# A smaller second selection, 16-bit look-ups, and 56 dense key rows for 64 in a one-core decoder layer

## The chip, the cores and the metric

The kernel runs on one core of a Trainium2 chip. Its time is the device time of one execution in microseconds (us). TensorE is the matmul engine; VectorE (DVE), ScalarE (ACT) and GpSimd (POOL) work beside it, SyncE (SP) issues plain transfers, and GpSimd issues the indirect ones (gathers by a list of row numbers).

## The reference

One post-norm decoder layer on 256 tokens of 2048 numbers: a projection, eight differential and eight stick-breaking attention heads, an output projection and a layer norm; then PEER, a retrieval of single-neuron experts; then a gated embedding. The change is in PEER:

```python
sa = jnp.einsum('thc,nc->thn', qa, sub_keys[0])        # 128 scores, first half key
sb = jnp.einsum('thc,nc->thn', qb, sub_keys[1])
va, ia = lax.top_k(sa, 16)
vb, ib = lax.top_k(sb, 16)
cand = va[..., :, None] + vb[..., None, :]             # 16 x 16 sums
top, sel = lax.top_k(cand, 16)                         # over 256 candidates
eidx = ia*128 + ib of the 16 chosen                    # expert number, 0..16383
gates = softmax(top)
act = gelu(einsum('thed,td->the', u[eidx], x))         # 8 heads x 16 experts a token
out = einsum('the,thed->td', gates * act, v[eidx])
```

`u` and `v` have 16384 rows of 2048 numbers (8 KB each), all of it in 32-bit floats.

## The kernel before, in words

**Two ways through PEER.** The first 88 tokens (64 + 16 + 8, `GROUPS`) are done "sparse": each of their experts' rows is gathered, 128 rows (1 MiB) to a gather, 88 gathers of `u` rows and 88 of `v` rows. VectorE forms the dot products (L986) and sums (L996). The other 168 tokens (`NDT`) are done with matmuls over blocks of 128 experts. An expert's number is ia*128 + ib, and the ia (key rows) are cut in two parts, `PARTS`: rows 0 to 63 are part 0, rows 64 to 127 part 1.

**The stages, in order of time.** (1) *query*: 16 products with `peer_wq`, scores, and the top 16 of the first token half (`topk_heads(0, ...)`), a head at a time. (2) *dense u*: for each of the `SEG1` = 64 key rows of part 0, `u_block` multiplies the whole 128-expert block of `peer_u` with the 168 tokens (L217) and keeps the gelu in `A0`/`A1`. Beside it the second token half's top 16 is found, the experts in use are counted (`first_flags`, `second_flags`, `count`), and lists of used experts are made (`list_work`). (3) *sparse u*: the used experts of part 1 are gathered by list, 128 to a block, transposed on TensorE (L1335) and multiplied (L1344). `CAPS` says how many blocks there are: 27 narrow ones, for experts that only the second half uses (128 columns), and 16 wide ones (168 columns). (4) *v*: the used experts of part 0 (27 + 17 blocks) and then of part 1 (27 + 16) are gathered from `v_rows` into `vf`, their weights from the table `s_w` into `wc` (L1305), and multiplied (`v_mm`, L1390). (5) *the seam and tail*: held blocks, the sparse tokens' sums brought in (`third_sums`, L1054; `v_out`, L1404; `res2`, L1462), the norm, the gate and the output.

**The gate pass.** `gate_work` builds, for three tokens at a time, one-hot matrices of ia and ib and multiplies them to a gate matrix per token (`product`, L1088 and L1089). The gates are scaled and split in two 16-bit parts: `hi` on ScalarE (L1079), `lo` on VectorE (L1080). Part 0's result multiplies `A0`/`A1` in place, which are then spilled to the table `s_w0`; the pass runs under sparse u. Part 1's result `G2` is made under part 0 of v, spilled to `s_w1`, and multiplied in `weigh` (L1413) with the gelu `WL`. A part-1 block's `wc` can be gathered only once `s_w1` is written (`done`). `G2` opens in the memory that `A0` and `A1` leave.

**What sets the order.** Side work is written as generators that yield; `run(work, n)` takes n steps between matmul blocks. `steps` is n in dense u. `gathers(n)` adds n to a sum and issues one sparse gather for each whole one, so the constants are gathers per block: `GQ` in query, `GU` in dense u until `second_flags` starts, `GUF` after it, `GUT` in its last ten blocks, `GUL` (narrow, wide) in sparse u, `GV` (narrow, wide) in v. Four buffers `gb` take the gathers. Reads of `wf`, `uf` and `vf` share five 1 MiB buffers, and row blocks are fetched up to `LEAD` = 4 blocks ahead. What a planner may not move is wrapped in `keep`; the rest it orders by its own model of durations.

**The first top 16 and the look-ups.** Per head, `top16` takes two MAX8, two FIND_INDEX8 and one MATCH_REPLACE8 over the 256 sums. The chosen position is split in i and j by shift and mask; then, per head and side, VectorE compares the positions with 0..15 (L731), GpSimd multiplies with the index list (L734), and VectorE adds up (L742, L744).

## Time and profile before

| | us |
|---|---|
| median of 3 runs | 1714.49 (1713.68 to 1715.63) |
| the profiled execution | 1712.57 |
| its span, first to last instruction | 1710.8 |
| TensorE busy / VectorE busy | 1612.1 / 1094.6 |
| query / dense u / sparse u | 414 to 534 / 534 to 853 / 853 to 1112 |
| v / seam and tail | 1112 to 1555 / 1555 to the end |

Durations are of the one profiled execution. A row of a group shows the count, the union of busy time and the mean of one in ns, then the engine's idle time just before these instructions and what ended it. Matmuls overlap, so the mean of one is longer than its step from start to start. A 32-bit matmul is two instructions.

### The profile page before, as it was taken

The page shows a single profiled execution, that of the slowest core. Times are in us where ns is not written, and L with a number is a line of the kernel's source. Part 1 is how long each engine was busy: PE and PEld are TensorE (multiplying, and loading weights), DVE is VectorE, ACT ScalarE, POOL GpSimd, SP SyncE. Part 2 cuts the span into 40 slices and gives each one's busy share as a digit, 9 for nine tenths or more (in the row PEclk, how much of TensorE's full clock was granted, in tenths as well). Part 3 has the DMA queues.
Part 4 walks back from the last instruction along what each step waited for, and adds up shares of the span by engine and source line. Part 5 has one row for each costly group of instructions (what it writes and reads, how often), then busy time and mean ns, then how long its engine had stood idle before and what let it go on. Part 6 is the DMA issues. An engine that isn't in the chain of part 4 may idle for free.

```text
span 1710.8 us, 29575 instructions
## 1 busy us (share of the span) xinstructions
PE 1612.1 (94%) x11176; PEld 1489.4 (87%) x11176; DVE 1094.6 (64%) x2430; ACT 717.9 (42%) x1666; POOL 718.1 (42%) x612
## 2 busy tenths in 40 slices
PE   9999999999999999999999999988897698984998
PEld 7888888877889999999999999978897688984786
DVE  5565488763599996656666867358672344544676
ACT  5677468753112654866366665313220000000552
POOL 0143023103266235111544655478886668871000
PEclk9999999999999999999999999989999899996999
DMA  7645644484998998988999999989999899996561
GB/s 294 197 151 166 234 154 160 159 315 156 379 361 319 379 364 344 408 334 310 364 421 391 350 344 345 412 348 373 398 409 413 319 419 414 387 413 230 175 262 50
DMA packets 94089, 531.26 MB, mean 311 GB/s; under 512 B 13257, under 2 KB 16649, under 8 KB 41465
## 3 DMA queue, kind: packets, MB, share of 16 engines
q0 software_dynamic: 49600, 329.36, 49.0%
q1 hardware_dynamic: 42612, 196.79, 31.3%
q10 hardware_dynamic: 1728, 3.15, 0.5%
q8 instruction: 90, 1.47, 0.3%
q14 instruction: 59, 0.48, 0.1%
HBM read 515.75 MB, written 16.08 MB: 311 GB/s over the span
## 4 chain that ended last, share of the span: by engine, by line
PE 71%; DMA 16%; issue 6%; POOL 3%; DVE 2%; ACT 1%; POOLq 0%; ACTq 0%; DVEq 0%; SPq 0%
PE ps_u L217 18%; PE ps_u L1344 8%; PE ps_qk L205 7%; DMA gb<-v_rows,eig 7%; PE ps_q L217 6%; PE ps_v L1390 5%; DMA vf<-v_rows,idxV 5%; PE ps_T L1335 4%; PE ps_qk L207 4%; DMA s_w<-A 2%; PE ps_v L224 2%; PE ps_v L226 2%; PE ps_v L225 2%; POOL wc L1305 2%; PE ps_gate L224 1%
## 5 line engine op out<-in xcount | busy, mean ns | idle before, releaser
L1390 PE MATMUL ps_v<-wc,vf 128*128 128x128 f32 (+1 forms) x2784 | 374.0, 295 | 57.6 <-DMA vf<-v_rows,idxV 26.0
L1390 PEld LDWEIGHTS ps_v<-wc,vf 128*128 128x128 f32 x2784 | 360.9, 197 | 64.4 <-DVE wc L1413 23.0
L217 PE MATMUL ps_u<-XF,wf 128*128 128x168 f32 x1888 | 291.4, 311 | 0.0
L996 DVE SCALAR_TENSOR_TENSOR y<-gb,ew,y 128x2048 f32<-128x2048 f32 x78 | 183.1, 2347 | 158.4 <-DMA gb<-v_rows,eig 158.3
L127 DVE TENSOR_TENSOR wl<-wf,wh 128x1024 fp32r<-128x1024 f32 (+1 forms) x199 | 212.7, 1091 | 104.3 <-ACT wh L126 103.1
L217 PEld LDWEIGHTS ps_u<-XF,wf 128*128 128x128 f32 x1888 | 271.4, 190 | 3.6
L126 ACT CAST wh<-wf 128x1024 fp32r<-128x1024 f32 (+1 forms) x199 | 172.1, 892 | 231.6 <-DMA wf<-ple_gate 117.6
L986 DVE SCALAR_TENSOR_TENSOR gb<-gb,xq 128x2048 f32<-128x2048 f32 x88 | 202.1, 2301 | 25.4 <-DMA gb<-u_rows,eig 22.7
L1344 PE MATMUL ps_u<-XF,uT 128*128 128x128 f32 (+1 forms) x1376 | 199.7, 289 | 0.0
L1020 POOL DMA_INDIRECT gb<-u_rows,eig x88 | 108.8, 1237 | 197.8 <-DVE eqb L857 69.7
L205 PE MATMUL ps_qk<-X,wh 128*128 128x512 f32 x512 | 185.2, 401 | 0.0
L1344 PEld LDWEIGHTS ps_u<-XF,uT 128*128 128x128 f32 x1376 | 178.9, 191 | 0.2
L1020 POOL DMA_INDIRECT gb<-v_rows,eig x88 | 134.9, 1533 | 58.7 <-issue 18.1
L207 PE MATMUL ps_qk<-X,wl 128*128 128x256 f32 x512 | 145.7, 285 | 0.0
L1079 ACT ACTIVATE hi<-eq,ghf 128x64 f16<-128x64 f16 x336 | 92.3, 339 | 121.5 <-DVE eq L857 111.1
L1338 ACT COPY uT<-ps_T 128x512 f32<-128x512 f32 x172 | 100.5, 586 | 97.9 <-PE ps_T L1335 95.1
L1305 POOL DMA_INDIRECT vf<-v_rows,idxV x87 | 118.6, 1363 | 48.6 <-issue 19.3
L1305 POOL DMA_INDIRECT wc<-s_w,idxW x87 | 117.6, 1351 | 40.7 <-issue 24.3
L205 PEld LDWEIGHTS ps_qk<-X,wh 128*128 128x128 f32 x512 | 96.4, 188 | 22.0 <-issue 1.0
L217 PE MATMUL ps_q<-XF,wf 128*128 128x256 f32 x512 | 113.8, 379 | 0.6 <-ACT eb L586 0.6
L217 PEld LDWEIGHTS ps_q<-XF,wf 128*128 128x128 f32 x512 | 95.8, 190 | 13.3 <-ACT eb L586 1.0
L1335 PE MATMUL ps_T<-ident,uf 128*128 128x128 f32 x688 | 103.8, 275 | 0.0
(342 smaller groups left out, 2550.9 us busy)
## 6 DMA issues: line engine op xcount, KB each, us to landing
wf<-peer_u SPq DMA_DIRECT2D x59, 1024.0 KB
wf<-w_qk SPq DMA_DIRECT2D x64, 512.0 KB
wf<-w_out SPq DMA_DIRECT2D x32, 512.0 KB
wf<-peer_wq SPq DMA_DIRECT2D x16, 1024.0 KB
wf<-ple_gate SPq DMA_DIRECT2D x16, 1024.0 KB
wf<-w_v SPq DMA_DIRECT2D x16, 512.0 KB
wf<-w_sv SPq DMA_DIRECT2D x15, 512.0 KB
s_w<-G SPq DMA_DIRECT2D x8, 672.0 KB
```

The source lines that it names most:

```text
L126: self.order(nc.scalar.copy(wh, src))
L127: self.order(nc.vector.tensor_tensor(wl, src, wh.bitcast(F32), op=ALU.subtract))
L205: nc.tensor.matmul(ps, wh[:, j * P:(j + 1) * P], xt[:, dt, :], start=dt == 0, stop=False)
L207: nc.tensor.matmul(ps[:, :T], wl[:, j * P:(j + 1) * P], xt[:, dt, :T], start=False, stop=dt == ND - 1)
L217: nc.tensor.matmul(ps[:, :T - t0], wf[:, dt * P:(dt + 1) * P], xt[:, dt, t0:], start=dt == 0, stop=dt == ND - 1)
L986: keep(nc.vector.scalar_tensor_tensor(g, g, 1.0, xq[i], op0=ALU.mult, op1=ALU.mult, accum_out=eact[i][:, j:j + 1]))
L996: keep(nc.vector.scalar_tensor_tensor(ys[i], g, ew[i][:, j:j + 1], ys[i], op0=ALU.mult, op1=ALU.add))
L1020: keep(nc.gpsimd.indirect_dma_start(out=g, out_offset=None, in_=a[kind], in_offset=bass.IndirectOffsetOnAxis(ap=eig[i][:, 0, j:j + 1], axi ...
L1305: keep(nc.gpsimd.indirect_dma_start(out=dst, out_offset=None, in_=src, in_offset=bass.IndirectOffsetOnAxis(ap=idx[:, b:b + 1], axis=0), bo ...
L1335: nc.tensor.transpose(ps[:, j * P:(j + 1) * P], uf[:, (4 * c + j) * P:(4 * c + j + 1) * P], ident)
L1344: nc.tensor.matmul(ps[:, :n], uT[:, j * P:(j + 1) * P], XF[:, d, NSP + c0:NSP + c0 + n], start=d == 0, stop=d == ND - 1)
L1390: return nc.tensor.matmul(o, vf[:, d * P:(d + 1) * P], wc[:, c0:c0 + n], start=False, stop=last and (d % 3 == 2 or d == ND - 1))
```

## The change

It has five parts.

1. Second selection: `a[i] + b[j]` of two sorted lists of 16. If (i+1)*(j+1) > 16, sixteen or more sums are at least as large, so only i < 3 with any j, and the other i with j < 4, are kept: 3 x 16 + 13 x 4 = 100 sums for 256. The position is decoded with shifts and a maximum.
2. Look-ups: for several heads in one go, in 16-bit floats, on VectorE alone: compare, multiply, and four adds that halve the list. The first token half is done in `BATCH`es of 1, 2, 2, 2, 1 heads for 8 single ones, the second all at once (29 yields for 34).
3. Counts: the count's bank is zeroed by a matmul first, so the first half's counts may be added at any time and run on beside the second half's. `steps` is 4 for 5, then 3.
4. The `lo` products of three tokens become one 16-bit operation.
5. Sizes and schedule: 56 dense key rows for 64; the part sizes and block counts that follow; part 1's gate pass is made ready at block 43 of sparse u's 48 and steps on there; in v the pass always takes 2 steps per half block; gather rates are changed; `wc` has 5 slots for 8 in part 0.

```diff
-SEG1 = 64
+SEG1 = 56
...
-CAPS = ((27, 17), (27, 16))
+CAPS = ((24, 15), (30, 18))
...
+CAND = ((0, 3, 16), (3, 16, 4))
+NCAND = sum((i1 - i0) * w for i0, i1, w in CAND)
+BATCH = ((0, 1), (1, 2), (3, 2), (5, 2), (7, 1))
...
-GQ = 1.6
-GU, GUF, GUT = 0.60, 0.85, 0.50
-GUL, GV = (0.95, 1.30), (0.62, 0.92)
+GQ = 1.7
+GU, GUF, GUT = 0.80, 0.92, 0.50
+GUL, GV = (1.00, 1.40), (0.66, 0.95)
...
+    def equal(dst, keys, vals, order=keep):
+        n, m = dst.shape[1], dst.shape[2]
+        shape = [P, n, m // 2, 2]
+        order(nc.vector.tensor_tensor(
+            dst.rearrange("p n (k two) -> p n k two", two=2),
+            pairs(keys)[:, None].to_broadcast(shape), vals[:, :, None, :].to_broadcast(shape),
+            op=ALU.is_equal))
...
+        for i0, i1, w in CAND:
+            shape = [P, n, i1 - i0, w]
+            c1 = c0 + (i1 - i0) * w
+            first(nc.vector.tensor_tensor(
+                cand[:, :n, c0:c1].rearrange("p h (i j) -> p h i j", j=w),
+                a[:, :, i0:i1, None].to_broadcast(shape), b[:, :, None, :w].to_broadcast(shape),
+                op=ALU.add))
+            c0 = c1
         for h in range(h0, h0 + n):
...
+            top16(tkl, CV[:, t, h, :], CI[:, t, h, :], cand[:, h - h0, :], first)
+            yield
...
+        for which, dst in ((0, iaN), (1, ibN)):
+            eq = tkl.tile([P, PH * TOPK, TOPK], F16, name="eqsel", tag="eqsel", bufs=1)[:, :nk]
+            equal(eq, io128[:, :TOPK], at[which], first)
+            e4 = eq.rearrange("p (h k) i -> p h k i", k=TOPK)
             first(nc.vector.tensor_tensor(
+                e4, e4, TIh[:, t, 2 * h0 + which:2 * h0 + 2 * n:2, None, :].to_broadcast(
+                    [P, n, TOPK, TOPK]), op=ALU.mult))
+            if n > 2:
+                yield
+            for w in (8, 4, 2):
+                first(nc.vector.tensor_tensor(eq[:, :, :w], eq[:, :, :w], eq[:, :, w:2 * w],
+                                              op=ALU.add))
+            first(nc.vector.tensor_tensor(dst[:, t, h0 * TOPK:(h0 + n) * TOPK], eq[:, :, 0],
+                                          eq[:, :, 1], op=ALU.add))
             yield
...
-        keep(nc.tensor.matmul(cnt[0][:, h * P:(h + 1) * P], ohb, eq, start=t in (NSP, P),
-                              stop=t in (P - 1, T - 1)))
+        keep(nc.tensor.matmul(cnt[0][:, h * P:(h + 1) * P], ohb, eq, start=False,
+                              stop=t == T - 1))
...
+        keep(nc.tensor.matmul(cnt[0], ident, zero.to_broadcast([P, 2 * P]), start=True,
+                              stop=False))
...
             next(gating, None)
+            next(flags, None)
             yield
...
-                keep(nc.vector.tensor_scalar(lo[:, j, :], eq[:, j, :], glf[:, t], None,
-                                             op0=ALU.mult))
+            shape = [P, n, ns // 2, 2]
+            keep(nc.vector.tensor_tensor(
+                lo[:, :n].rearrange("p n (k two) -> p n k two", two=2),
+                eq[:, :n].rearrange("p n (k two) -> p n k two", two=2),
+                gl2[:, t0:t0 + n, None, :].to_broadcast(shape), op=ALU.mult))
...
-        gathers(1 if ia < EARLY else GU if steps == 1 else GUF if ia < SEG1 - 10 else GUT)
+        gathers(0.9 if ia < EARLY else GU if steps == 1 else GUF if ia < SEG1 - 10 else GUT)
...
-        wc = wpool.tile([P, NDT], F32, name="wc", tag="wc", bufs=NWC)
+        wc = wpool.tile([P, NDT], F32, name="wc", tag="wc", bufs=LEAD + 1 if wpool is wcp else NWC)
...
             wcp = pools.open("wcp", "right", bufs=1)
+            work = gate_work(ohp, (G2,), *PARTS[1], 1, True)
...
-            if 2 <= b < NBLK[1] - 5 and (c or n > P):
+            if b >= 2 and (c or n > P):
                 run(work, 1)
...
-    work = gate_work(ohp, (G2,), *PARTS[1], 1, True)
...
-            done = run(work, 2 if n > P or d > 8 else 1)
+            done = run(work, 2)
```

More of the change, by code (lines that the diff above doesn't have):

```diff
@@ L722, in topk_heads @@
-        nc.vector.tensor_single_scalar(CJ[:, t, hs], CI[:, t, hs], 15, op=ALU.bitwise_and)
-        nc.vector.tensor_single_scalar(CI[:, t, hs], CI[:, t, hs], 4, op=ALU.logical_shift_right)
-        nc.vector.tensor_copy(CIf[:, t, hs], CI[:, t, hs])
-        nc.vector.tensor_copy(CJf[:, t, hs], CJ[:, t, hs])
-        yield
-        late = []
-        for which, pos, dst in ((0, CIf, iaN), (1, CJf, ibN)):
-            for h in range(h0, h0 + n):
-                eq = tkl.tile([P, TOPK, TOPK], F32, name="eq", tag="eqsel", bufs=4)
-                first(nc.vector.tensor_tensor(
-                    eq, pos[:, t, h, :, None].to_broadcast([P, TOPK, TOPK]),
-                    io128f[:, None, :TOPK].to_broadcast([P, TOPK, TOPK]), op=ALU.is_equal))
-                nc.gpsimd.tensor_tensor(
-                    eq, eq, TIf[:, t, 2 * h + which, None, :].to_broadcast([P, TOPK, TOPK]),
-                    op=ALU.mult)
-                late.append((dst[:, t, h * TOPK:(h + 1) * TOPK], eq))
-                if h % 2:
-                    yield
-                if len(late) > 2:
-                    o, e = late.pop(0)
-                    nc.vector.tensor_reduce(o, e, axis=AX.X, op=ALU.add)
@@ L743, in topk_heads @@
-        for o, e in late:
-            nc.vector.tensor_reduce(o, e, axis=AX.X, op=ALU.add)
-        yield
+        a, b = (TV[:, t, 2 * h0 + which:2 * h0 + 2 * n:2] for which in range(2))
+        cand = tkl.tile([P, PH, NCAND], F32, name="cand", tag="cand", bufs=1)
+        c0 = 0
+        for i0, i1, w in CAND:
[6 more added lines that the diff above has]
+            c0 = c1
@@ new lines, in topk_heads @@
+        for h in range(h0, h0 + n):
+            top16(tkl, CV[:, t, h, :], CI[:, t, h, :], cand[:, h - h0, :], first)
+            yield
+        ci = CI[:, t, hs].rearrange("p h k -> p (h k)")
+        s4, s2 = (tkl.tile([P, PH * TOPK], U32, name=nm)[:, :nk] for nm in ("by16", "by4"))
+        pF, u1 = (tkl.tile([P, PH * TOPK], F32, name=nm)[:, :nk] for nm in ("pF", "u1"))
+        at = [tkl.tile([P, PH * TOPK, 2], F16, name=f"at{which}")[:, :nk] for which in range(2)]
+        two = [P, nk, 2]
@@ new lines, in topk_heads @@
+        first(nc.vector.tensor_copy(TIh[:, t, 2 * h0:2 * h0 + 2 * n],
+                                    TI[:, t, 2 * h0:2 * h0 + 2 * n]))
+        first(nc.vector.tensor_single_scalar(s4, ci, 4, op=ALU.logical_shift_right))
+        first(nc.vector.tensor_single_scalar(s2, ci, 2, op=ALU.logical_shift_right))
+        first(nc.vector.tensor_copy(pF, ci))
+        first(nc.vector.scalar_tensor_tensor(
+            at[0], s2[:, :, None].to_broadcast(two), -9.0, s4[:, :, None].to_broadcast(two),
+            op0=ALU.add, op1=ALU.max))
@@ L798, in topk_work @@
         nc.vector.tensor_copy(io128, io128f)
-        for h in range(PH):
-            for _ in topk_heads(0, h, 1):
-                pass
-            head_slots(h)
+        for h0, n in BATCH:
+            for _ in topk_heads(0, h0, n):
+                pass
+            for h in range(h0, h0 + n):
+                head_slots(h)
             yield
@@ L807, in topk_work @@
         second, first, flags = topk_heads(1, 0, PH), gates(0), first_flags()
-        for step in range(24):
-            next(second)
+        for step, _ in enumerate(second):
             if step > 2:
@@ L813, in topk_work @@
             yield
-        for _ in second:
-            next(flags, None)
-            yield
-        for _ in range(9):
-            next(flags, None)
-            yield
-        for _ in flags:
-            yield
+        for _ in first:
+            pass
         yield from index_T(1)
-        yield from second_flags(gates(1))
+        yield from second_flags(gates(1), flags)
     def index_T(t):
@@ L922, in second_flags @@
                 counts()
+        for _ in flags:
+            yield
         while made:
@@ L1189, in list_work @@
         if part:
-            steps = 5
+            steps = 3
         yield
@@ L1268, in build @@
             iaT, ibT = (lsp.tile([P, T, 2], F16, name=nm) for nm in ("iaT", "ibT"))
[L1269 removed]
+            ghf = lsp.tile([P, T], F32, name="ghf")
+            gl2 = lsp.tile([P, T, 2], F16, name="gl2")
             a0p = pools.open("a0p", "right", bufs=1)
@@ L1276, in build @@
         query(hh)
-        if hh % 2 == 0 and hh:
+        if hh in [2 * (h0 + n) for h0, n in BATCH]:
             run(work, 1)
```

40 lines of the change are left out of this document (17 added, 23 removed).

## The prediction

> **What bounds the kernel now.** I read the page first: the busy shares and the slices.
>
> ```profile
> span 1710.8 us, 29575 instructions
> ...
> PE 1612.1 (94%) x11176; PEld 1489.4 (87%) x11176; DVE 1094.6 (64%) x2430; ACT 717.9 (42%) x1666; POOL 718.1 (42%) x612
> ...
> PE   9999999999999999999999999988897698984998
> ...
> PEclk9999999999999999999999999989999899996999
> DMA  7645644484998998988999999989999899996561
> ```
>
> TensorE is full up to slice 26; nearly all of its idle time lies in slices 26 to 37. The DMA engines are nearly full from slice 10 on. So the list of what TensorE waited for says which of the two is short there:
>
> ```profile
> PE ps_v L1390 <- DMA vf<-v_rows,idxV: 26.0, 15, 5.1
> PE ps_v L1390 <- DVE wc L1413: 18.6, 5, 12.9
> PE ps_y L1462 <- DVE XF L1404: 17.2, 2, 16.1
> PE ps_G L1088 <- DVE lo L1080: 6.4, 1, 6.4
> PE ps_v L1390 <- issue: 5.5, 5, 1.5
> PE ps_v L1390 <- PEq L1521: 4.5, 1, 4.5
> ```
>
> All six belong to the second half of the retrieval: v blocks (L1390), the gate pass under them (L1088) and their end (L1462). By stage (columns: stretch, length, busy time of PE, weight load, DVE, ACT, POOL, then granted clock, DMA share, GB/s; query, dense u, sparse u, v in two pieces, the seam to the tail):
>
> ```profile
> 414.00:534.00 120.00, 119.39 (x591) 105.62 (x590) 84.36 (x270) 17.25 (x42) 58.48 (x62) 1.00 0.89 344
> 534.00:853.00 319.00, 319.00 (x2378) 311.62 (x2377) 236.18 (x628) 179.09 (x540) 105.44 (x133) 1.00 0.90 352
> 853.00:1112.00 259.00, 259.00 (x2397) 256.85 (x2396) 171.36 (x468) 149.98 (x388) 131.48 (x88) 1.00 0.97 378
> 1112.00:1303.00 191.00, 170.45 (x1569) 165.37 (x1568) 129.44 (x365) 46.17 (x168) 153.53 (x109) 0.97 0.97 384
> 1303.00:1555.00 252.00, 205.05 (x1526) 199.48 (x1525) 102.81 (x97) 6.72 (x12) 174.01 (x129) 0.94 0.97 393
> 1555.00:1606.00 51.00, 33.26 (x173) 30.23 (x174) 27.53 (x46) 9.02 (x20) 5.74 (x6) 0.70 0.43 134
> ...
> 1376.00:1480.00 104.00, 92.69 (x783) 90.22 (x784) 46.19 (x53) 4.54 (x8) 80.10 (x59) 1.00 1.01 415
> ```
>
> Both u stages run TensorE without a gap and have DMA share left (0.10 and 0.03). The v stage is short of DMA: share 0.97, TensorE idle 67 us of 443. So a byte moved out of v into u is worth time while u can carry it, and PE work saved in u is worth time directly.
>
> **The change, part by part.** *Blocks.* A dense block is 32 matmul instructions of 168 columns. A sparse block is 16 transposes and 32 instructions, in 128 (narrow) or 168 (wide) columns. From the chain of waits:
>
> ```profile
> 684.55 4.62 PE ps_u L217 x32
> 1253.44 4.64 PE ps_v L1390 x32
> 1444.85 3.81 PE ps_v L1390 x32
> ```
>
> Eight dense blocks fewer: -8 x 4.62 = -37 us. Sparse u goes from 27+16 to 30+18 blocks. The sparse stage took 259 us for 43 blocks, 6.0 each with a gate pass in it; matmuls alone bound a block below by 3.8 or 4.6. With the transposes I take 5.3 (narrow) and 6.3 (wide), as the pass must fit into the 6.0 too: 3 x 5.3 + 2 x 6.3 = +28.5. The v stage has 39+48 = 87 blocks as before, 54 narrow and 33 wide both times. Net in u: **-8 us**, 5 less MB-sized reads being 3 (8 dense, 5 row blocks).
>
> *Gathers.* Each moves 1 MiB (128 rows of 8 KB), 176 in all, and the loops hand them out at GQ, GU, GUF, GUT, GUL and GV per block. I counted the generators' yields: the step where GU ends moves from block 30 to 21. Before, issued by the end of query, dense u, sparse u: 20.8, 66.2, 112.7. After: 22.1, 67.4, 122.6. So v gets 53.4 instead of 63.4. At GV 0.66/0.95 its 39 part-0 blocks take 30.1 and 30 narrow part-1 blocks 19.8, and the rest is gone four wide blocks later: at block 73 of the 84 before the held ones. Before, 2.3 were left after block 84 and were run off in a row, which is the 16.1 us wait for XF.
>
> *Can u carry it?* Dense u moved 352 x 319 = 112 MB; eight blocks less is 104 MB in 319 - 37 = 282 us: 369 GB/s. Sparse u moved 98 MB; five more blocks and 8.7 more gathers make 112 MB in 290 us: 385 GB/s. Rows above show 378 without a gap in TensorE and 415 at share 1.01, so it fits barely. I put **+4 us** for stalls (between 0 and the 21 us of the second rival).
>
> The Trainium skill speaks against this part: its page "DMA: Bandwidth & Descriptors" (Specifications) gives about 358 GB/s as the HBM limit of one core, below the 435 of the fabric. By that, u's 216 MB would take 603 us and not 572, an estimate of 31 us lost. The 415 GB/s of the row above disagrees, so I don't use it.
>
> *v stage.* Before: 384 x 191 + 393 x 252 = 172 MB. After: 10 gathers less (10.5 MB) and 0.7 MB more table (72 rows for 64): 162 MB. From block 73 on v is bound by TensorE: 11 wide blocks x 4.64 = 51 us. By then the reads are five blocks ahead, so all but some 13 MB (9 blocks of 1.14 MB, and weights of the next stage) came before it, at 405 GB/s, between the 393 and 415 of the rows: 149 / 405 = 368 us. Sum 419, against 443 now: -24. The same sum gives 426 for before, where 443 was measured, so 17 us there were not bandwidth. They are the late second pass: its 64 x 168 table is spilled only when v block 38 or so ends, and part 1's wc gathers can't start before. The pass needs 125 yields; 20 now run in u, and at 4 a block the rest ends near v block 26, eight blocks ahead of its first reader. I leave 6 of the 17: v **-18 us**.
>
> *Seam.* The rest of the XF wait goes too, less 2 us for the first result: **-14**. Behind it TensorE ran at 0.70 of its clock for 51 us:
>
> ```profile
> 1571.00 0.69 PE L1462 MATMUL ps_y<-ident,XF 128*128 128x128 f32 x2 [16.10 <-DVE XF L1404]
> ...
> 1571.69 13.49 PE ps_y L1054 x64
> ```
>
> 64 small matmuls took 13.5 us there. With the array kept busy the seam's 33 us of PE work at 0.70 would be about 25: **-8**. If the branch check (PEq, 4.5 us, stays) already lowers the clock, 0.
>
> *VectorE.* Its rows for what goes, and for what is like the new forms:
>
> ```profile
> L680 DVE MAX8 CV<-cand 128x8 f32<-128x256 f32 x16 | 6.8, 428 | 0.3
> ...
> L680 DVE MAX8 TV<-S 128x8 f32<-128x128 f32 x32 | 9.1, 284 | 24.8 <-ACT S L701 24.8
> ...
> L731 DVE TENSOR_TENSOR eq<-CJf,io128f 128x256 f32<-128x256 f32 x16 | 10.1, 637 | 0.0
> ...
> L742 DVE TENSOR_REDUCE iaN<-eq 128x16 f32<-128x256 f32 x8 | 3.2, 406 | 0.0
> ...
> L857 DVE TENSOR_TENSOR ohb<-io,ibT 128x384 f16<-128x384 f16 x108 | 37.7, 349 | 0.0
> ...
> L857 DVE TENSOR_TENSOR eq<-io,iaT 128x192 f16<-128x192 f16 x108 | 26.7, 247 | 0.0
> ...
> L1080 DVE TENSOR_SCALAR lo<-eq,glf 128x64 f16<-128x64 f16 x326 | 57.3, 255 | 0.0
> ```
>
> MAX8 costs 1.1 ns an element (428 and 284), so 253 ns at 100: five such operations a head save 0.9 us, 7 us per token half. Compare-and-reduce cost 16 x (0.6 + 0.4) = 16 us per half; a 16-bit operation costs 0.53 ns an element (349 and 247), so 2048 elements 1.2 us, and two rounds of compare, multiply and four adds 8 us. That is about 15 us of VectorE and 16 of POOL per half. If the multiply by a broadcast list ran at twice that, 2.4 us less. The lo products become one operation of 216 elements, 0.26 us for 3 x 0.255: 0.5 us x 112 groups = 57 us, over both passes. None of this is on the path: no TensorE wait in u names VectorE. I count it as **0**. What uses it up: the same 45 gathers, of 2.3 us each, in a dense stage 37 us shorter, and 4 pass steps per narrow v block for 3. Without that cover VectorE would be at 236 of 282 us in dense u, still under.
>
> *The rest, 0.* The bank zeroed for any-order counts is two matmul instructions (below 1 us). The first half's flags (ACT) now run partly beside the second's; see the third rival. The wc pool of part 0 has 5 slots for 8: vf has 5 too, so a pair still waits for the same block; three early wc issues of 1.35 us go, 4 us either way. Behind a waiting wc stand vf and the gathers on POOL. Part 1's first G writes, new in u, must wait for the part-0 spill reading that memory, and VectorE's gather sums stand behind them:
>
> ```profile
> 1077.26 31.47 DMA s_w<-A
> ```
>
> The spill now starts near block 39 or 40 and G2 is first written about block 44, 25 us later; the wait is 0 to some 10 us, under five blocks of prefetch, so 0.
>
> **Sum.** -8 + 4 - 18 - 14 - 8 = -44. The profiled execution took 1712.6 (span 1710.8 and 1.8 around it): 1668.6. The median of the runs is 1.9 above it, so **1670**.
>
> **Rivals.** *DMA full in u (20%).* u is bound at 365 GB/s, between its 352 and 378: 216 / 365 = 593 us, +21 for +4; v goes on at the 393 of its own row, 149 / 393 + 51 = 430, so -13 less the same 6 left over: about -7. Sum -8 + 21 - 7 - 14 - 8 = -16: 1698. For it: demand of 385 where 378 stood at 0.97. Against: 415 in the last row.
>
> *Everything fits (10%).* No stall in u, all 17 us of v's delay gone, reads at 415: -8 - 33 - 14 - 8: 1651.
>
> *The lists come late (10%, slower).* ACT's first flags take 57 us:
>
> ```profile
> L865 ACT ACTIVATE dist<-io,nibT 128x128 f16<-128x128 f16 x40 | 16.0, 401 | 1.2
> ...
> L866 ACT ACTIVATE oa<-dist 128x128 f16<-128x128 f16 x40 | 12.4, 310 | 11.2 <-PE ps_cnt L870 10.4
> ...
> L866 ACT ACTIVATE ob<-dist 128x128 f16<-128x128 f16 x40 | 12.3, 308 | 1.1
> ```
>
> (two dist each, 40 tokens: 32 + 12.4 + 12.3.) Interleaved with the second half's, they hold back the counts; the lists are in the program by block 50 of 56, a margin of 6 x 4.6 = 28 us. If the chain of counts and lists slips by the whole 57 and by the 37 of cover taken away, TensorE stands 94 - 28 = 66 us at the first row block. Against the 44 won that is +22: 1736 on the runs' scale. It decides from a slip above 72 us. Against: VectorE and ACT have 83 and 140 us idle in that stage, the second half's selection is shorter, and matmuls of u may go ahead of counts.
>
> *No change (5%).* The u stalls and the late pass eat all: within 0.2%, which is about what a measurement of this kernel can tell from no change: 1714.
>
> **How the numbers follow.** Forecast 55%, the rivals 20, 10, 10, 5. Faster 0.85, same 0.05, slower 0.10. The range takes in the second and the best case and the ends of the unknown costs (clock 0 or -8, prefetch, wc): 1647 to 1706; slower and same are mostly left out.
>
> **What would show it.** Sparse u starting near 816 us instead of 853, 290 us long, with no wait for DMA above 1 us: right in u; waits for wf or uf there: the second rival. No wait above 3 us for wc L1413 or for XF L1404, the last gather of v_rows some 50 us before the last v block, and a clock near 1 in the seam show the v and seam terms. A long wait at the first row transposes (L1335's successor) or at counts shows the lists late. I am wrong if v is not shorter although its gathers end early.

## The result, and the profile after

The changed kernel takes 1698.66 us (1696.82 to 1699.17, 4 runs) where the kernel before takes 1714.09 (1711.54 to 1715.63): a ratio of 0.991, 95% interval 0.9892 to 0.9927. It is faster, by 15.4 us; 44 had been forecast. The profiled execution took 1699.17, its span 1697.4.

The page of the changed kernel: the span, the busy shares, and three of the 40-slice rows.

```profile
span 1697.4 us, 29309 instructions
...
PE 1608.6 (95%) x11162; PEld 1485.0 (87%) x11162; DVE 1041.8 (61%) x2216; ACT 723.3 (43%) x1684; POOL 697.4 (41%) x586
...
PE   9999999999999899999999999899977988889998
...
PEclk9999999999999999999999999899998999999999
DMA  8544644484997799999899999999998999986561
```

TensorE now has short slices (14 and 26) in the two u stages, where it had none. What it waited for, from the list of waits of TensorE (us in total, times, longest):

```profile
PE ps_v L1411 <- DMA vf<-v_rows,idxV: 29.3, 15, 8.6
PE ps_v L1411 <- DVE wc L1434: 13.2, 7, 7.1
PE ps_G L1111 <- ACT hi L1099: 9.6, 2, 5.9
...
PE ps_gT L855 <- DVE iaN L774: 2.8, 1, 2.8
...
PE ps_gT L855 <- DVE ibN L774: 1.6, 1, 1.6
...
PE ps_y L1483 <- DVE XF L1425: 1.1, 1, 1.1
```

The long wait for `XF`, 16.1 us, is gone; the short one of 1.1 us behind it was there before too. New are the waits for `hi` and for the index lists `iaN` and `ibN`; the v blocks still wait for `vf` and `wc`. By stage (query, dense u, sparse u, v in two pieces, seam; columns as in the prediction's table):

```profile
414.00:537.00 123.00, 121.83 (x588) 107.52 (x589) 70.59 (x256) 17.18 (x42) 42.07 (x49) 0.97 0.85 328
537.00:829.00 292.00, 284.01 (x2123) 276.65 (x2122) 228.32 (x650) 173.49 (x533) 89.82 (x116) 0.99 0.93 365
829.00:1133.00 304.00, 293.98 (x2687) 291.25 (x2686) 186.83 (x404) 169.05 (x445) 172.20 (x111) 0.97 0.97 382
1133.00:1330.00 197.00, 170.85 (x1474) 165.15 (x1473) 106.91 (x211) 38.33 (x136) 143.79 (x104) 0.95 0.95 370
1330.00:1556.00 226.00, 197.90 (x1542) 193.01 (x1541) 87.94 (x95) 4.43 (x8) 157.65 (x119) 0.98 0.95 381
1556.00:1592.00 36.00, 34.23 (x206) 31.22 (x207) 18.08 (x42) 11.21 (x24) 2.15 (x4) 0.86 0.52 157
```

To compare kernels I cut every trace at the first matmul of each stage (first `ps_q` product, first dense `ps_u`, first `ps_T` transpose of a row block, first `ps_v` of the retrieval, first `ps_gate`), and counted the gathers that POOL had issued by the first `ps_v`. All lengths below are made in this way.

| us | query | dense u | sparse u | v and seam | rest | gathers before v |
|---|---|---|---|---|---|---|
| before | 119.4 | 318.6 | 264.1 | 489.7 | 104.9 | 108 |
| after | 122.6 | 291.3 | 307.4 | 456.3 | 105.2 | 123 |
| difference | +3.2 | -27.3 | +43.3 | -33.3 | +0.3 | +15 |
| forecast | 0 | -37 (+ part of 4) | +28.5 (+ part of 4) | -40 | 0 | +10 |

The differences sum to -13.8 (another 0.4 lies ahead of query). So the v half did most of what was forecast, and u gave 20 us of it back: it became 16 us longer and not 4.5 shorter.

### The profile page after: what moved, and what is told of

Same layout as the page of the kernel before. It is cut to its first block, busy times and chain, and to the rows that moved or that the text cites. A ratio compares the mean times of both kernels' runs of the same rounds, so it can differ in the third digit from the quotient of the medians.

```text
span 1697.4 us, 29309 instructions
## 1 busy us (share of the span) xinstructions
PE 1608.6 (95%) x11162; PEld 1485.0 (87%) x11162; DVE 1041.8 (61%) x2216; ACT 723.3 (43%) x1684; POOL 697.4 (41%) x586
## 5 line engine op out<-in xcount | busy, mean ns | idle before, releaser
L220 PE MATMUL ps_u<-XF,wf 128*128 128x168 f32 x1632 | 250.7, 310 | 0.0
L220 PEld LDWEIGHTS ps_u<-XF,wf 128*128 128x128 f32 x1632 | 235.2, 191 | 3.1 <-issue 0.2
L1368 PE MATMUL ps_u<-XF,uT 128*128 128x128 f32 (+1 forms) x1536 | 226.1, 292 | 0.4 <-ACT uT L1362 0.4
L1368 PEld LDWEIGHTS ps_u<-XF,uT 128*128 128x128 f32 x1536 | 203.2, 194 | 1.0 <-ACT uT L1362 0.7
L1040 POOL DMA_INDIRECT gb<-v_rows,eig x88 | 148.1, 1683 | 44.0 <-issue 17.9
L1362 ACT COPY uT<-ps_T 128x512 f32<-128x512 f32 x192 | 111.6, 586 | 98.8 <-PE ps_T L1359 95.7
L1099 ACT ACTIVATE hi<-eq,ghf 128x56 f16<-128x56 f16 (+1 forms) x336 | 92.3, 339 | 81.8 <-DVE eq L714 79.9
L1329 POOL DMA_INDIRECT vf<-v_rows,idxV x87 | 103.9, 1194 | 53.9 <-PE ps_v L1411 23.7
L1359 PE MATMUL ps_T<-ident,uf 128*128 128x128 f32 x768 | 115.5, 276 | 0.0
L1329 POOL DMA_INDIRECT uf<-u_rows,idxV x48 | 68.4, 1426 | 100.4 <-PE ps_T L1359 92.6
```

The source lines that it names most:

```text
L220: nc.tensor.matmul(ps[:, :T - t0], wf[:, dt * P:(dt + 1) * P], xt[:, dt, t0:], start=dt == 0, stop=dt == ND - 1)
L1040: keep(nc.gpsimd.indirect_dma_start(out=g, out_offset=None, in_=a[kind], in_offset=bass.IndirectOffsetOnAxis(ap=eig[i][:, 0, j:j + 1], axi ...
L1329: keep(nc.gpsimd.indirect_dma_start(out=dst, out_offset=None, in_=src, in_offset=bass.IndirectOffsetOnAxis(ap=idx[:, b:b + 1], axis=0), bo ...
L1359: nc.tensor.transpose(ps[:, j * P:(j + 1) * P], uf[:, (4 * c + j) * P:(4 * c + j + 1) * P], ident)
L1368: nc.tensor.matmul(ps[:, :n], uT[:, j * P:(j + 1) * P], XF[:, d, NSP + c0:NSP + c0 + n], start=d == 0, stop=d == ND - 1)
```

## The experiments

The theory after the first look: u is not short of bytes; it loses its time where VectorE, which takes its instructions in order, stands at a gather's sum with short instructions behind it that TensorE needs at once. The rivals: DMA is full in u (the second rival of the prediction), or the lists come late (the third).

**Where the gate pass starts.** The pass of part 1 put back to the start of v; and, in a second kernel, the pass left where the change has it, but no gathers handed out around its start (blocks 39 to 45 of 48).

```diff
# e1_pass_at_v
-            work = gate_work(ohp, (G2,), *PARTS[1], 1, True)
...
-            if b >= 2 and (c or n > P):
+            if 2 <= b < NBLK[1] - 5 and (c or n > P):
...
+    work = gate_work(ohp, (G2,), *PARTS[1], 1, True)
# e8_no_gather_at_seam
-        gathers(GUL[n > P])
+        if not NBLK[1] - 9 <= b < NBLK[1] - 2:
+            gathers(GUL[n > P])
```

> The changed kernel with one edit undone: part 1's gate pass is made ready when v begins, as before the change, and takes no step in sparse u. Theory A (order of queues): the two waits of TensorE for hi in sparse u (5.9 and 3.8 us) and the slow clock behind them (0.76 from 1084 to 1120) come from these steps, because VectorE stands at a gather sum when the one-hot of the pass is due. Then sparse u falls from 304 to about 290 us, and v gets a wait of some 6 us at its beginning, as the kernel before had (6.4 for lo): in all 1690 to 1699. Theory B (the DMA engines are full in sparse u): sparse u stays near 304, v gets longer by the 20 steps of the pass and the wait: 1702 to 1710.

> The changed kernel without sparse gathers beside blocks 39 to 45 of sparse u (some 10 gathers move to v). In the late-fetch run GpSimd's order did not change: five wc gathers still stood ahead of the sparse ones and waited 6.7 us for the spill, so it could not tell. Here no sparse gather is under way when the one-hots of the second pass are due. Theory A (VectorE stands at the sum of a sparse gather, and the pass behind it): the two waits of TensorE for the pass in sparse u go and sparse u falls from 306 to 293 to 297 us; v and the seam get longer by the moved gathers, as with the old rates: 1700 to 1712 in all. If the one-hots are late for another cause (ScalarE, or the spill itself before G2 is written), the waits stay and sparse u stays above 302.

Sparse u took 294.0 us in the first and 290.4 in the second (307.4 in the changed kernel; 290 was forecast). Ratios to before: 0.9856 (0.9823 to 0.989) and 0.9883 (0.9858 to 0.9908): v and the seam gave back 6.7 and 17.4 us, with 5 and 11 gathers more left for them. The timeline of VectorE in the changed kernel shows the place (start, duration, instruction, idle time before it and what ended it):

```profile
1083.97 2.35 DVE L1016 SCALAR_TENSOR_TENSOR y<-gb,ew,y 128x2048 f32<-128x2048 f32 x1 [5.79 <-DMA gb<-v_rows,eig]
...
1091.79 2.35 DVE L1016 SCALAR_TENSOR_TENSOR y<-gb,ew,y 128x2048 f32<-128x2048 f32 x1 [2.58 <-DMA gb<-v_rows,eig]
...
1094.14 0.27 DVE L714 TENSOR_TENSOR eq<-io,iaT 128x216 f16<-128x216 f16 x1
```

and of TensorE:

```profile
1085.79 2.30 PE L1368 MATMUL ps_u<-XF,uT 128*128 128x168 f32 x15
...
1094.84 0.22 PE L1111 MATMUL ps_G<-hi,ohb 128*128 128x72 f16 x1 [5.88 <-ACT hi L1099]
...
1095.80 2.61 PE L1368 MATMUL ps_u<-XF,uT 128*128 128x168 f32 x8 [0.19 <-ACT uT L1362]
```

VectorE waited for gathered rows, summed them, and only then made the one-hot `eq` (0.27 us of work) from which ScalarE makes `hi`. TensorE had the pass's product next, so u's own matmuls came behind it, and ran at half speed (8 in 2.61 us, where 15 took 2.30). The Trainium skill, "PSUM — Partial Sum Buffer" (Engine vs sequencer instructions), states that VectorE's queue is strictly first in, first out and that matmuls start in program order; the rows agree, as `eq` and u's matmuls each come right behind what was late. The window from 1084 to 1120 had a granted clock of 0.76:

```profile
1084.00:1120.00 36.00, 25.98 (x172) 24.90 (x172) 22.58 (x37) 12.87 (x37) 20.92 (x15) 0.76 0.88 350
```

These 36 us hold 10.0 us without a matmul and 36 x 0.24 = 8.6 us of clock not granted. Together that is 18.6, and sparse u is 18.3 us above the 289.1 of a kernel without the wait (f2, below). Nearly half of the price is the clock.

Without those gathers (e8) the wait is gone and the pass costs u nothing that shows. The first product of the pass in e8, on TensorE:

```profile
1087.56 0.20 PE L1111 MATMUL ps_G<-hi,ohb 128*128 128x72 f16 x1
```

That leaves POOL: five `wc` gathers stood ahead of the row gathers on its queue, the first of them waiting for the spill of `s_w0` (POOL, changed kernel).

```profile
1070.00 0.94 POOL L1040 DMA_INDIRECT gb<-v_rows,eig  x1 [0.30 <-issue]
...
1087.81 2.29 POOL L1329 DMA_INDIRECT wc<-s_w,idxW  x1 [7.16 <-DMA s_w<-A]
```

The next row gather was issued at 1098.58. By count, the sum that VectorE began at 1091.79 is of the gather issued at 1070.00, before POOL stood at the spill. So this stop can't have made the first wait; it can have had a part in the second, 3.76 us at 1109.35.

**POOL's share in it.** The `wc` gathers handed out two blocks later.

```diff
# e7_late_fetch
-        if b >= NBLK[1] - 4:
+        if b >= NBLK[1] - 2:
```

> The changed kernel with the first v block fetched two blocks later in sparse u (from block 46 of 48 for 44). In the changed kernel the first wc waits 7.2 us on GpSimd for the spill of part 0, and the sparse gathers behind it land late; VectorE stands at their sums, with the one-hot of the pass behind. Theory A: the spill has landed when wc is issued, the two waits for hi (5.9 and 3.8 us) shrink and sparse u falls by 6 to 13 us; v may begin with a wait of up to 5 us for vf: 3 to 12 us less than the changed kernel. Theory B (DMA full in sparse u): no change in sparse u, and 0 to 5 us more at the start of v.

Inconclusive: the planner still put five `wc` gathers ahead of the row gathers, POOL waited 6.65 us for the spill, TensorE 4.0 and 3.6 us; ratio 0.989 (0.9867 to 0.9912). A later run, f1_gq_160 (below), answered it: there `wc` did not wait on POOL at all, and TensorE stood as long, 9.33 us in one wait for 9.6 in two (POOL, then TensorE, of f1_gq_160).

```profile
1072.16 1.00 POOL L1329 DMA_INDIRECT wc<-s_w,idxW  x1 [0.30 <-issue]
```

```profile
1089.53 0.22 PE L1111 MATMUL ps_G<-hi,ohb 128*128 128x72 f16 x1 [9.33 <-ACT hi L1099]
```

So the spill's wait is not what makes it; VectorE's order is.

**The rates.** All five rates as before; then GU alone; then GQ alone.

```diff
# e3_old_rates
-GQ = 1.7
-GU, GUF, GUT = 0.80, 0.92, 0.50
-GUL, GV = (1.00, 1.40), (0.66, 0.95)
+GQ = 1.6
+GU, GUF, GUT = 0.60, 0.85, 0.50
+GUL, GV = (0.95, 1.30), (0.62, 0.92)
...
-        gathers(0.9 if ia < EARLY else GU if steps == 1 else GUF if ia < SEG1 - 10 else GUT)
+        gathers(1 if ia < EARLY else GU if steps == 1 else GUF if ia < SEG1 - 10 else GUT)
# e9_gu_060
-GU, GUF, GUT = 0.80, 0.92, 0.50
+GU, GUF, GUT = 0.60, 0.92, 0.50
# f1_gq_160
-GQ = 1.7
+GQ = 1.6
```

> The changed kernel with the gather rates of the kernel before (1.6; 1 for the first blocks; 0.60, 0.85, 0.50; 0.95 and 1.30; 0.62 and 0.92), everything else as changed. By the sum of the prediction some 10 gathers go back from u to v and gathers are left over at the end, so v and the seam are 18 to 30 us longer and u is at most 4 us shorter: 1712 to 1725. If DMA in u is what made u longer than forecast (theory B), u is 15 to 25 us shorter and the whole within 5 us of the changed kernel: 1694 to 1704.

> The changed kernel with 0.60 gathers per block in the first dense blocks for 0.80, every other rate as changed. With all old rates dense u had no wait and took 282 us, as forecast, and with the new ones 291 with waits for the index lists; flags started later only moved the wait (6.9 us at 647). If VectorE is full there (77 of 80 us from 575 to 655) because of the gathers brought forward, dense u falls to 282 to 284 with this one rate, and three gathers move on to later stages: 1686 to 1694 against 1695 of the changed kernel beside it. If the later rate (0.92) or the look-ups themselves are the cause, dense u stays at 289 to 292.

> The changed kernel with GQ 1.6 (rate of row gathers under the query) as before and nothing else: 22.1 - 20.8 = 1.3 gathers fewer by the end of the query stage. Theory A (the gather sums that queue on VectorE at the start of dense u stand in front of the look-ups of the last heads of the first token half, so the index lists come late): no waits for iaN or ibN above 0.5 us near 560 to 570 us, dense u 282 to 284 us for 291, ratio to the kernel before 7 to 9 us better than the changed kernel's 0.989 to 0.991, so about 0.984 to 0.986. Theory B (the dense stage is late from the rates GU and GUF of u itself): dense u stays 290 to 292 with both waits, ratio 0.988 to 0.991.

Dense u: 281.9, 290.7 and 282.9 us (291.3 in the changed kernel; 282 was forecast). Ratios 0.9929 (0.991 to 0.9948), 0.9875 (0.9848 to 0.9902) and 0.983 (0.9788 to 0.9871). One tenth of a gather per step of query, 1.3 gathers in all, costs dense u 8.4 us: TensorE's idle time in it is 8.0 us in the changed kernel and 2.7 in f1 (0.7 and 1.3 us of them waits for the second half's lists). It holds in every trace with 56 rows: 281.9 to 283.0 us in the five kernels with GQ 1.6, 288.6 to 292.0 in the eleven with 1.7. The end of the first half's look-ups in the changed kernel, on VectorE:

```profile
552.60 2.28 DVE L1006 SCALAR_TENSOR_TENSOR gb<-gb,xq 128x2048 f32<-128x2048 f32 x1
...
555.11 2.28 DVE L1006 SCALAR_TENSOR_TENSOR gb<-gb,xq 128x2048 f32<-128x2048 f32 x1
...
557.56 2.27 DVE L1006 SCALAR_TENSOR_TENSOR gb<-gb,xq 128x2048 f32<-128x2048 f32 x1
...
560.47 0.19 DVE L774 TENSOR_TENSOR iaN<-eqsel 128x16 f32<-128x16 f16 x1
...
565.34 2.29 DVE L1006 SCALAR_TENSOR_TENSOR gb<-gb,xq 128x2048 f32<-128x2048 f32 x1 [3.55 <-DMA gb<-u_rows,eig]
...
567.78 0.19 DVE L774 TENSOR_TENSOR ibN<-eqsel 128x16 f32<-128x16 f16 x1
```

and in f1_gq_160:

```profile
554.11 0.19 DVE L774 TENSOR_TENSOR iaN<-eqsel 128x16 f32<-128x16 f16 x1
...
555.69 0.18 DVE L774 TENSOR_TENSOR ibN<-eqsel 128x16 f32<-128x16 f16 x1
```

Four dot products of gathered rows, one of them late by DMA, stand inside the last batch's look-ups; `ibN` is done 12 us later than with GQ 1.6, and TensorE waits for both lists (2.76 and 1.62 us). It is the same mechanism as in sparse u. All old rates win 9 us in dense u and leave sparse u at 304.9 with 10 gathers fewer, so bytes are not what makes that stage long; in v and seam they lose 20 us (476.6).

**What v loses by.** Two kernels: part 1's `wc` pool with 5 slots for 8, as part 0 has; and a lower GV, which spreads the remaining gathers over all of v.

```diff
# e5_wc5
-        wc = wpool.tile([P, NDT], F32, name="wc", tag="wc", bufs=LEAD + 1 if wpool is wcp else NWC)
+        wc = wpool.tile([P, NDT], F32, name="wc", tag="wc", bufs=LEAD + 1)
# e6_level_v
-GUL, GV = (1.00, 1.40), (0.66, 0.95)
+GUL, GV = (1.00, 1.40), (0.55, 0.85)
```

> The changed kernel with 5 slots for wc in part 1 too, for 8. In the changed kernel eight wc gathers stand in a row on GpSimd from 1286 to 1300 when part 1's pool opens, ahead of the vf that TensorE waits 8.6 us for. Theory A (order on GpSimd's queue): with 5 slots at most five stand in a row, the 8.6 us wait and the slow clock behind it shrink: 5 to 9 us less than the changed kernel. Theory B (the DMA engines are full in v, and the order doesn't matter): within 2 us of the changed kernel.

> The changed kernel with 0.55 and 0.85 gathers per v block for 0.66 and 0.95, so that the gathers last until the end of v. In the changed kernel the DMA share is 1.01 from 1330 to 1516 and 0.66 from 1516 to 1556. If DMA bounds the middle of v, some 7 gathers moved out of it save 7 x 1.05 MB / 0.41 = 18 us there, and the later end costs part of it: 5 to 14 us less than the changed kernel. If waits for order bound v, as its length of 414 to 427 us in all kernels so far suggests, within 3 us of it. If the last gathers come too late, the seam's wait for XF returns (16 us in the kernel before).

> The changed kernel itself once more, as the measure for the runs beside it: 0.991 of the kernel before, with the same waits (5.9 and 3.8 us for hi in sparse u, 8.6 us for vf near 1310, 7.1 us for wc near 1517).

The three ran on one chip: 1687.1, 1690.24 and, for the changed kernel, 1695.22 us; ratios to before 0.985 (0.9828 to 0.9873), 0.9859 (0.9838 to 0.9879) and 0.9889 (0.9869 to 0.991). With 8 slots POOL issues eight `wc` gathers in a row when the fetches of part 1 begin, ahead of the `vf` gather that TensorE needs (POOL, first and last of the eight; then TensorE), in the changed kernel:

```profile
1286.14 1.01 POOL L1329 DMA_INDIRECT wc<-s_w,idxW  x1 [0.31 <-issue]
...
1298.43 2.44 POOL L1329 DMA_INDIRECT wc<-s_w,idxW  x1 [0.31 <-issue]
```

```profile
1310.41 3.98 PE L1411 MATMUL ps_v<-wc,vf 128*128 128x168 f32 x13 [8.60 <-DMA vf<-v_rows,idxV]
```

The changed kernel, traced again, has the same two stops of the pass in sparse u, once put down to `lo` (5.0 us) and once to `hi` (4.5). With 5 slots the wait of 8.60 is gone (the longest for `vf` is 4.0) and v and seam are 449.1 us. Levelling moves the gathers: v is 19 us shorter, the seam 13 us longer, since the last gather goes out at 1525.6 (1504.4 in the changed kernel) and a long wait for `wc`, whose multiplication stands behind the gather sums on VectorE, opens there; 450.6 together. From the waits of TensorE in e6_level_v:

```profile
PE ps_v L1411 <- DVE wc L1434: 14.8, 2, 11.7
```

How full v is, in the changed kernel, from 1330 us in three windows:

```profile
1330.00:1472.00 142.00, 121.31 (x1024) 117.75 (x1023) 59.70 (x57) 4.43 (x8) 113.39 (x82) 1.00 1.01 413
1472.00:1516.00 44.00, 37.64 (x264) 36.55 (x263) 24.57 (x28) 0.00 (x0) 34.63 (x27) 0.98 1.02 415
1516.00:1556.00 40.00, 38.95 (x256) 38.70 (x257) 3.67 (x12) 0.00 (x0) 9.63 (x11) 0.93 0.66 234
```

The DMA engines are full until the last gathers are in, and stand a third idle in the 40 us behind. Over all 18 traced kernels v and seam together fall on one line: 489.7 us with 108 gathers issued before v, 463.3 with 117, 456.3 with 123, a least-squares slope of 2.0 us per gather, with each kernel within some 7 us of the line. The kernels differ in more than the gathers, so the slope is a fit and no price measured alone: e3, e8 and e9 against the changed kernel give 2.0, 1.6 and 0.7 us per gather, f3 and f4 against f2 (below) 2.8 and 2.5. By bytes, 1.05 MB at 413 GB/s would be 2.5 us.

**The other parts.** 64 dense rows for 56, all else as changed; the first half's flags begun later; `lo` by one product a token; the old selection and look-ups.

```diff
# e4_64_rows
-SEG1 = 56
+SEG1 = 64
...
-CAPS = ((24, 15), (30, 18))
+CAPS = ((27, 17), (27, 16))
# e2_flags_later
-            next(flags, None)
+            if step > 7:
+                next(flags, None)
# e10_lo_by_one
...
-            shape = [P, n, ns // 2, 2]
-            keep(nc.vector.tensor_tensor(
...
+            for j in range(n):
+                keep(nc.vector.tensor_scalar(lo[:, j, :], eq[:, j, :], glf[:, t0 + j:t0 + j + 1], None,
+                                             op0=ALU.mult))
# e11_old_selection
-BATCH = ((0, 1), (1, 2), (3, 2), (5, 2), (7, 1))
+BATCH = tuple((h, 1) for h in range(8))
...
+                nc.gpsimd.tensor_tensor(
+                    eq, eq, TIf[:, t, 2 * h + which, None, :].to_broadcast([P, TOPK, TOPK]),
+                    op=ALU.mult)
```

> The changed kernel with 64 dense key rows and the old block counts (27+17 and 27+16), everything else as changed. By the block sum dense u is 37 us longer and sparse u 28.5 us shorter: u 8 us longer, and v starts 8 us later with as many gathers left as the rates then leave (some 4 less done in sparse u, 7 more in dense u): 1700 to 1709. Theory A adds that the part-0 pass has as little room as before (it is flushed at block 38 of 43), so TensorE's wait at the beginning of part 1's pass may be longer. If the block trade costs time, this kernel is faster than the changed one: below 1696.

> The changed kernel with the first half's flags started eight steps of the second selection later, everything else the same. Theory A: the waits of TensorE for the transposes of the index lists (2.8 and 1.6 us at 558 and 567) and the slow blocks behind them (9 and 7 us for 4.6) go, because the look-ups of the last batch are done by then: dense u 291 to about 283, 1690 to 1693 in all. Theory B (dense u is long because its transfers fill the DMA engines, share 1.01 from 575 to 655): the waits go but the time is given back at later loads: 1697 to 1701.

> The changed kernel with the old lo products (three operations of one token each, 32-bit scalars, for one operation of three tokens). The prediction counted this part at nothing: 57 us more of VectorE over both passes, under cover. If so, within 3 us of the changed kernel. If VectorE's order at the waits is what counts, the second pass starts later by some 0.5 us a group and the waits for hi and lo get longer: 3 to 10 us more.

> The changed kernel with the old second selection and look-ups (256 sums, one head at a time, 32-bit, multiplied on GpSimd), everything else as changed. The prediction counted the new ones at nothing on the path, 15 us of VectorE per token half. If VectorE is full in the first dense blocks (theory A), the 15 us come back there: the waits for the index lists and the counts grow by 10 to 25 us and the whole is 1705 to 1720. If it has room, within 4 us of the changed kernel.

With 64 rows: ratio 0.9976 (0.9956 to 0.9996); dense u 329.0, so 37.7 more than the changed kernel for 8 blocks, and sparse u 281.4 for 307.4. The trade of blocks is worth what was forecast for dense u; sparse u's share can't be read off, as that kernel has a single wait of 18.2 us for `lo` in it. Later flags: 0.9868 (0.9838 to 0.9898), dense u 290.4: the waits near 560 us are gone, but one of 6.9 us for `iaN` stands at 647, where the second half's lists are due, so the loss was only moved. `lo` one by one: 0.9907 (0.9877 to 0.9938), against 0.9889 and 0.991 for the changed kernel. Old selection: 0.9888 (0.9854 to 0.9923). Neither of the VectorE savings can be told from nothing in time. The one trace of the old selection has a sparse u of 314.2 us, with short stops for the lists at its start and one of 10.0 us for `lo`, and a dense u of 288.6.

**All causes taken out.** If these causes are separate, removing them should bring the forecast back. GQ is 1.6 and part 1's `wc` has 5 slots in all three kernels; f2 and f4 have the pass at v as e1 has, f3 has the pass in u with the gap in the gathers as e8 has.

```diff
# f2_all_causes, beside the edits of e1, e5 and f1
-GUL, GV = (1.00, 1.40), (0.66, 0.95)
+GUL, GV = (1.00, 1.40), (0.60, 0.88)
# f3_gather_gap, beside the edits of e8, e5 and f1
-GUL, GV = (1.00, 1.40), (0.66, 0.95)
+GUL, GV = (1.00, 1.40), (0.68, 0.98)
# f4_old_u_rates, beside the edits of e1, e5 and f1
-GU, GUF, GUT = 0.80, 0.92, 0.50
-GUL, GV = (1.00, 1.40), (0.66, 0.95)
+GU, GUF, GUT = 0.60, 0.85, 0.50
+GUL, GV = (1.00, 1.40), (0.64, 0.93)
...
-        gathers(0.9 if ia < EARLY else GU if steps == 1 else GUF if ia < SEG1 - 10 else GUT)
+        gathers(1 if ia < EARLY else GU if steps == 1 else GUF if ia < SEG1 - 10 else GUT)
```

> The changed kernel with every cause found so far taken out: GQ 1.6, part 1's gate pass begun at the start of v (with yields 5 and 4 to a block as in the earlier run of that kind), 5 wc slots for part 1, GV 0.60 and 0.88 between the changed kernel's 0.66 and 0.95 and the levelled 0.55 and 0.85. If the causes are separate their sizes add: dense u -8, sparse u -13, v and seam -7 (wc slots) and -3 to -5 (level), +5 for the pass put back into v: 26 to 28 us under the changed kernel, ratio 0.973 to 0.975, near the forecast's 0.974. If they share one cause (bytes: what one stage no longer waits for is waited for in the next), v grows by what u gains and the ratio stays 0.982 to 0.985.

> As the last, but with the pass left in sparse u and no gathers handed out in the seven blocks where it starts (so that no gather sum stands in front of its one-hots), GV 0.68 and 0.98 for the 7 to 8 gathers that this pushes into v. Separate causes: sparse u 290, dense u 282 to 284, v 413 to 420, seam 37 to 45: ratio 0.970 to 0.974. One shared cause (bytes): the gathers pushed out come back as v and seam longer by 12 to 17 us as in the earlier run without these gathers, ratio 0.980 to 0.985.

> As the second, but also with u's dense rates as before (0.60, 0.85, 1 in the first blocks), so 6 to 7 gathers fewer in dense u, and GV 0.64 and 0.93 for them. If GQ is what held the dense stage up: dense u 282 as in the second, v and seam 5 to 9 us longer, ratio 0.976 to 0.980. If GU or the first blocks' rate is: dense u 282 here and 290 in the second, and this one the faster of the two.

| | ratio to before | dense u | sparse u | v and seam | gathers before v |
|---|---|---|---|---|---|
| f2 | 0.9752 (0.971 to 0.9795) | 282.9 | 289.1 | 463.3 | 117 |
| f3 | 0.9838 (0.9795 to 0.988) | 283.0 | 289.3 | 480.3 | 111 |
| f4 | 0.982 (0.9778 to 0.9862) | 282.2 | 289.5 | 473.4 | 113 |

f2 is the fastest kernel of this study: 1678.62 us where before took 1720.85 in the same comparison, 42 us less (f4, the next beside it, 1689.02; the two intervals overlap a little). Its two u stages and the two pieces of v, by window:

```profile
536.00:819.00 283.00, 280.26 (x2120) 274.24 (x2118) 220.62 (x634) 172.80 (x532) 86.21 (x112) 1.00 0.93 369
819.00:1108.00 289.00, 288.87 (x2647) 285.65 (x2646) 170.68 (x363) 161.42 (x414) 159.29 (x109) 1.00 0.97 384
1108.00:1330.00 222.00, 194.14 (x1658) 187.19 (x1657) 127.77 (x259) 46.95 (x168) 166.67 (x115) 0.94 0.95 376
1330.00:1536.00 206.00, 180.83 (x1397) 176.61 (x1396) 89.49 (x95) 6.61 (x12) 150.61 (x114) 0.96 0.98 398
```

Both u stages stand at the forecast's 282 and 290, sparse u at 384 GB/s without a gap: the u causes are separate and bytes are not among them. f3 and f4 are as good in u and lose 17 and 10 us in v and seam, with 6 and 4 gathers more left for it; the line's 2.0 us each would be 12 and 8. So bytes are the one cause that is shared, as f3's expectation had it for the second case, and it acts in v. Old GU on top of GQ 1.6 (f4) wins under 1 us in dense u: GQ was what held that stage up.

That f2's 42 us are so near the forecast's 44 is in part luck. Between the traces it is 34.7 us, since the before of the same comparison ran slower than the profiled one. The split is another one too: u gives 10.7 us (4.5 forecast) and v and seam 26.4 (40 forecast). And f2's own expectation was missed in v: with the sizes found one by one v and seam should have come to 449 to 451 us, and they took 463.3. v had 6 gathers more left than in the changed kernel, which the line puts at 12 us.

## Why the prediction was wrong, step by step

Between the traces some 31 us of the forecast are missing: 20.5 in u, 6.7 in v and seam, 3.2 in query, the rest outside the stages.

**Blocks: right.** -37 and +28.5 were forecast; f2, whose u has next to none of these waits, shows -35.7 and +25.0.

**"Can u carry it?", +4: the question was right, the means were wrong.** It was put to the DMA engines alone. They carry it: dense u 369 and sparse u 384 GB/s in f2, against 369 and 385 worked out. What u couldn't carry is a gather whose sum stands on VectorE ahead of what TensorE needs next. That took 8.4 us in dense u (f1) and 13 to 17 in sparse u (e1, e8). It is the step that failed.

**"The wait is 0 to some 10 us, under five blocks of prefetch, so 0": the sentence where it failed.** The prediction named the start of part 1's pass and that gather sums stand behind it, and set it off against row blocks fetched ahead. Fetched blocks are no cover: TensorE had its rows, but the product of the pass ahead of them in its queue. What is late was also named the wrong way round: not the sums behind the pass, but the pass behind the sums. Before, the same wait (`lo`, 6.4 us) stood in v, which the prediction's first table shows; it was moved, not removed.

**VectorE, counted as 0: right as a price, wrong as a cover.** The prices held: MAX8 over 100 took 256 ns (253 worked out), `lo` of 216 elements 264 ns (260), a 16-bit compare of 2048 and a multiply by a broadcast list 1224 ns each (1.2 us, and not twice that). From the groups of VectorE in the changed kernel, in dense u and then in sparse u:

```profile
L680 DVE MAX8 CV<-cand 128x8 f32<-128x100 f32 x16 | 3.8, 256 | 0.1
...
L766 DVE TENSOR_TENSOR eqsel<-eqsel,TIh 128x2048 f16<-128x2048 f16 x2 | 2.4, 1224 | 0.1
```

```profile
L1101 DVE TENSOR_TENSOR lo<-eq,gl 128x216 f16<-128x216 f16 x56 | 14.8, 264 | 0.0
```

And undoing them changed nothing measurable (e10, e11). "VectorE would be at 236 of 282 us, still under" was a mean over a stage, and says nothing of single waits. At 561 to 565, inside the first half's look-ups, VectorE stood idle for 3.55 us behind a gather that had not landed. From 575 to 655, where the second half's lists are made, it is full (window of the changed kernel; VectorE is the third busy time, 77.16 of 80):

```profile
575.00:655.00 80.00, 80.00 (x571) 78.73 (x570) 77.16 (x230) 51.42 (x152) 25.22 (x38) 1.00 1.01 412
```

**v, -18 and the 17 us of a late pass: the size came near, the cause was not there.** The 419 us worked out for v end with block 84, and in the trace v took 419.8 us to that point. But the 443 that they were set against reach to 1555, and before block 84 ended at 1537.4, after 421.1 us. Behind it, up to the wait for `XF`, come 17.5 us with held blocks and two waits (TensorE, before):

```profile
1541.84 1.46 PE L1390 MATMUL ps_v<-wc,vf 128*128 128x168 f32 x4 [4.48 <-PEq L1521]
...
1548.37 6.54 PE L1390 MATMUL ps_v<-wc,vf 128*128 128x168 f32 x32 [5.06 <-DMA vf<-v_rows,idxV]
```

That stretch is as long as the 17 us which the prediction laid to a late second pass; it shrank to 5.7 us. In all, 13 us were saved up to the `XF` wait, 5 fewer than forecast. Up to block 84, v became only 1.3 us shorter although its gathers end early, which the prediction had named as the sign of being wrong. e1, f2 and f4 have the pass in v again and lie 2.2, 3.9 and 1.6 us below the common line: no cost of running it there shows. v and the seam together follow the gathers left, and those were miscounted. The yields gave 112.7 by the end of u, while POOL had issued 108, 88 of `u_rows` and these (issues of the kernel before up to its first `ps_v`; least, median and longest in ns, then the first and last start):

```profile
L1020 POOL DMA_INDIRECT gb<-v_rows,eig x20: 937/966/3092, 987.2 to 1090.2; - x20
```

The changed kernel had issued 88 and 35. So 15 gathers left v where 10 had been counted, and at the line's 2.0 us each they are worth 30 of the 33 us; nearly all of it is saved behind block 84, where before ran off its last gathers. "From block 73 on v is bound by TensorE" was right, and a loss: the last gather went out at 1504.4, 51 us ahead of block 84's end, as forecast, and the DMA engines stood at 0.66 in those 40 us after being full. Gathers bunched ahead of that point make TensorE wait.

**"A pair still waits for the same block; 4 us either way": mis-sized.** Part 0's slots did no harm, but the 8 that stayed in part 1 cost 7 us (e5). The prediction spoke of part 0 only.

**Seam, -14 and -8: right in their sum.** From the last matmul ahead of the `XF` wait to the gate, TensorE took 51.0 us before and 30.8 after, 20 less: the 16.1 us of the wait and 4 us of faster matmuls, half of the 8. The granted clock went from 0.70 (1555 to 1606) to 0.86 (1556 to 1592), not to 1.

**The rivals.** The second one's 1698 is the measured time by luck, and its 593 us for u and -29 for v and seam are near the 599 and -33 of the table. Its cause, full DMA engines in u, is not what the runs show: f2 moves 384 GB/s through sparse u without a gap, and f1 has dense u short with 1 or 2 gathers less. The lists did come late in dense u, but by 4.4 us of waits and not by 66, and because of dots (f1); flags begun later won nothing (e2). By the 358 GB/s that the prediction names from the Trainium skill, "DMA: Bandwidth & Descriptors" (Specifications), u would have been bound; the windows show 412 to 415 over 44 to 142 us at a share of 1.01 to 1.02, so not that, again.

**What stays open.** Query took 122.3 to 122.6 us in seven of the 18 traced kernels, this one among them, and 119.2 to 120.3 in the others. The 3 us are clock: in the seven the granted clock was 0.66 in the ten us from 414 on, in ten of the others 1.00 (first the changed kernel, then the one before):

```profile
414.00:424.00 10.00, 8.83 (x35) 7.25 (x36) 1.63 (x3) 3.95 (x9) 4.43 (x4) 0.66 0.30 116
```

```profile
414.00:424.00 10.00, 9.39 (x51) 7.94 (x50) 2.44 (x5) 4.39 (x9) 8.25 (x10) 1.00 0.29 110
```

Why the clock fell there is open: kernels with the same GQ are on both sides (f4 119.7, f1 122.3), and the wait ahead of it is 1.1 us in the changed kernel and 1.2 in e1, which kept its clock. These 3 us belong to no term of the prediction. The wait for `hi` was not removed by an order of VectorE's queue with the one-hots first; only taking the gathers or the pass away was tried.

## What to carry to other kernels

When work is moved beside other work, ask which in-order queues both pass through and what each instruction there waits for: a share of busy time below 1 says nothing about a 0.3 us instruction behind one that waits for a transfer. Cover counts only if it lies in front of the waiting instruction on the same queue; blocks fetched ahead are none if the stalled product comes first. Where a stage is bound by bytes, price a moved transfer once (some 2 us per MiB here, by the fit) and count what was really issued by then in the trace, not what the program's rates hand out.
